# Tree attention on one core: K and Q of 40 more heads are regrouped by GpSimd before they are transposed, and ScalarE takes over eight V copies

## The chip, the cores and the metric

The kernel runs on one core of one Trainium2 chip. The metric is the device time of one execution in microseconds (us); lower is better. A core has five engines that run their own instruction streams and meet at semaphores: TensorE (PE in the profile; its weight loads are PEld), VectorE (DVE), ScalarE (ACT), GpSimd (POOL) and SyncE (SP). Transfers between the chip's memory and the core's on-chip memory are started by an engine (here nearly all by GpSimd) and carried by 16 DMA engines.

## The reference

The inputs Q, K and V have shape 8 x 12 x 512 x 64 (float32), so there are 96 heads of 512 rows. The 512 positions are the nodes of a binary heap, and a query may look at itself and at its ancestors only:

```python
for i in range(seq):
    mask[i, i] = 1
    parent = i
    while parent > 0:
        parent = (parent - 1) // 2
        mask[i, parent] = 1
scores = np.einsum('bhqd,bhkd->bhqk', Q, K) * scale + (1 - mask) * (-1e9)
weights = np.exp(scores - np.max(scores, axis=-1, keepdims=True))
weights = weights / (np.sum(weights, axis=-1, keepdims=True) + 1e-10)
return np.einsum('bhqk,bhkd->bhqd', weights, V).astype(np.float32)
```

## The kernel before

**Tiling.** A query has at most nine ancestors, so the kernel does not compute 512 x 512 scores. The keys are put in an order in which one tile of 128 keys holds the top of the tree (`scores1`, L507) and four further tiles hold what single groups of queries can see (`scores2`, L566). The mask is not added: code vectors of keys and queries are multiplied into the same PSUM sum first, so that a forbidden pair comes out very negative. The 96 heads are worked on as 48 pairs, i = 0 to 47. The pairs from i = 8 on are "wide": their K and Q were loaded with two heads in one transfer row, and two pairs (four heads) are transposed together.

**One step.** The main loop (L796) has one step for each i. Its order of work is written out by hand: the strings of `FIRST` (L792) for steps 0 to 8, then "SVK" in odd steps and "SVQ" in even ones. S is `scores1` and `scores2` of pair i: matmuls on TensorE and exponentials on ScalarE (L529 or L525 for the first tile, then L560 or L586). V is `values` of pair i-1 (L592, matmuls on L605 into the tile `ob`), followed by `norm` (L644): a reciprocal (L651) and a multiplication (L653) on VectorE. `ob` has one buffer, so the next `values` waits until `norm` is done. K and Q are `turn` (L497): TensorE transposes four heads of K or Q, and VectorE copies the result from PSUM (three copies for K on L470, L474 and L478, one for Q on L493). A turn runs some four pairs ahead of the scores that use it.

**Two ways to transpose.** K and Q come in blocks of 8 heads, b = 0 to 11. `turn_slot` (L437) transposes one of eight slots of a group of four heads. Where a block is not "laid", it issues two transposes with 64 columns of weights each (L450), straight from the loaded tile. Where it is laid, GpSimd has copied the two heads of a pair side by side into a tile `besideK` or `besideQ` (`lay`, L426, one copy for each of the two groups of a block, L433), and one transpose with 128 columns of weights does (L441). `besideK` and `besideQ` have one buffer for each group: the copy for the next block waits until TensorE has read the group. `LAID` (L139) lists the laid blocks: 8 to 11, heads 64 to 95.

**The order inside `values`.** For each pair there are 20 matmuls: 12 with 128 columns of weights ("firsts" and "wholes") and 8 with 64 columns ("halves"). Up to i = 27 the halves come last (L637 on). From i = `4 * LAID[0] - 4` = 28 they stand between firsts and wholes (L630).

**V.** V comes in blocks of 16 heads, o = 0 to 5. Its rows are rearranged from the loaded tile `vst` into `vt` by many small copies (`spread`, L311, all on L364). From o = 2 on, VectorE does the parts A, B, C and E (table `BY_VECTOR`, L733, one a step), and GpSimd does X, N, Z0, Z1 (`spread_pool`) and the four "top" parts 6 to 9 (`spread_top`, L369). ScalarE has a table of its own, `BY_SCALAR` (L754), used for o = 0 and 1 only; its copies come at the end of a step, behind the exponentials of that step.

**GpSimd's queue.** `pool_program` (L676) is one list, which GpSimd works through strictly in order: loads (`load_k` and `load_q` through L256 or L244, `load_rows` L285, `load_leaves` L294), copies, lays and stores (L662). `ready` (L712) only decides behind which step of the main loop an entry is put into the program. An entry that has to wait holds up everything behind it in the list. The loads convert float32 to bfloat16 on the way. The last four heads are stored by SyncE (L826).

Of the kernel before, what the change touches and what calls it, by code (L numbers as in the profile page):

```python
# [119 lines left out]
def kernel(  # L120
# [7 lines left out]
    nc = tc.nc  # L128
# [7 lines left out]
    WIDE = 8  # L136
    KB, VB, VO = 8, 16, 16
    EIGHT = 2
    LAID = (8, 9, 10, 11)  # L139
    assert NH % VB == 0  # L140

    fp32 = mybir.dt.float32
# [90 lines left out]
    issued = {(name, h) for name in ("kst", "qst") for h in (0, 1)}  # L233
# [35 lines left out]
    def head(i, a):  # L269

        return 2 * i + a if i < WIDE else 4 * (i // 2) + i % 2 + 2 * a
# [151 lines left out]
    def slots(st, i):  # L423
        return st[2 * i // KB].rearrange("p (g x) t d -> p g (x t) d", x=2)

    def lay(name, b):  # L426

        st = {"kst": ksts, "qst": qsts}[name][b]
        assert all((name, h) in issued for h in range(KB * b, KB * b + KB))
        laid[name, b] = two = beside[name[0].upper()]  # L430
        for g in range(KB // 4):
            src = st[:, 4 * g:4 * g + 4, :, :].rearrange("p (a x) t d -> p (x t) a d", x=2)
            nc.gpsimd.tensor_copy(  # L433
                out=two[:, g, :, :, :].bitcast(int32), in_=src.bitcast(int32)
            )

    def turn_slot(dst, name, i, s, out):  # L437

        two = laid.get((name, 2 * i // KB))
        if two is not None:  # L440
# [5 lines left out]
            return  # L446
        assert 2 * i // KB not in LAID
        st = slots({"kst": ksts, "qst": qsts}[name], i)
# [143 lines left out]
    def values(i):  # L592

        if i < NP - 1:
            obs[i] = ob = psO.tile([P, 2, 512], fp32, name="ob")
        else:
            obs[i] = ob = psS.tile([P, 2, 512], fp32, name="s1")
        e1, e2, vt = ets[i], e2s[i % NE], vts[(head(i, 0) // VB) % NV]

        vtile = VTILE if i < WIDE else WVTILE  # L600
        parts = EIGHT_PARTS if head(i, 0) >= VB * EIGHT else PARTS[i >= WIDE]
        assert all(("vt", n, head(i, a)) in issued for n in parts for a in range(2))

        def product(e, a, t, tile_v, lo=0, hi=128, **flags):
            nc.tensor.matmul(  # L605
                out=ob[lo:hi, a, 65 * t:65 * t + 65],
                lhsT=e[:, a, PLACE[t], lo:hi],
                rhs=vt[vtile[tile_v][0]][:, head(i, a) % VB, vtile[tile_v][1], 0:D + 1],
                **flags,
            )  # L610

        def firsts(a):
            for t in range(4):
                product(e1, a, t, 0, start=t == 0, stop=False)

        def halves(a, last=True):
            for t in (0, 1):
                product(e2, a, t, 1 + SELF[t], 0, 64, start=False, stop=last and t == 1)
                product(e2, a, t, 1 + t, 64, 128, start=False, stop=last and t == 1)

        def wholes(a, last=False):
            for t in (2, 3):
                product(e2, a, t, 1 + t, start=False, stop=last and t == 3)

        if i == NP - 1:
            for a in range(2):
                firsts(a)
                wholes(a)
                halves(a)
        elif i >= 4 * LAID[0] - 4:  # L630
            for a in range(2):
                firsts(a)
            for a in range(2):
                halves(a, False)
            for a in range(2):
                wholes(a, True)
        else:  # L637
            for a in range(2):
                firsts(a)
                wholes(a)  # L640
            for a in range(2):
                halves(a)
# [33 lines left out]
    def pool_program():  # L676

        ops = [
            (load_k, 2, 2), (load_q, 2, 2), (load_v, 0, 4), (load_v, 4, 4),
            (load_k, 4, 4), (load_q, 4, 4), (load_k, 8, 4),  # L680
            (load_q, 8, 4), (load_v, 8, 8), (load_k, 12, 4),
            (load_q, 12, 4), (load_k, 16, 8), (load_q, 16, 4), (load_rows, 1, "upper"),
            (load_rows, 1, "even"), (load_rows, 1, "odd"), (load_q, 20, 4),
            (load_k, 24, 8), (load_q, 24, 8), (load_rows, 2, "upper"),
            (load_k, 32, 8), (load_leaves, 2, 0), (load_leaves, 2, 1),
            (load_q, 32, 8), (load_rows, 3, "upper"),
            (spread_pool, (1, "Z0", 8, 16), (1, "Z1", 8, 16)),
            (load_k, 40, 8), (load_q, 40, 8), (load_leaves, 3, 0), (load_leaves, 3, 1),
            (spread_top, 2, 0, 16), (spread_pool, (2, "Z0", 0, 16), (2, "Z1", 0, 16)),
            (load_q, 48, 8), (spread_pool, (2, "X", 0, 16)),  # L690
            (load_k, 48, 8), (spread_pool, (2, "N", 0, 16)),
            (load_rows, 4, "upper"), (spread_top, 3, 0, 16),
            (load_k, 56, 8), (load_q, 56, 8), (load_leaves, 4, 0), (load_leaves, 4, 1),
            (spread_pool, (3, "X", 0, 16), (3, "N", 0, 16), (3, "Z0", 0, 16), (3, "Z1", 0, 16)),
            (load_k, 64, 8), (store_rows, 0, 2), (load_q, 64, 8), (store_rows, 2, 4),
            (load_k, 72, 8), (spread_top, 4), (store, nc.gpsimd, 4, 12), (lay, "kst", 8),
            (load_q, 72, 8), (spread_pool, (4, "X", 0, 16), (4, "N", 0, 16)),
            (lay, "qst", 8), (load_rows, 5, "upper"),
            (spread_pool, (4, "Z0", 0, 16), (4, "Z1", 0, 16)),
            (load_leaves, 5, 0), (load_leaves, 5, 1), (load_k, 80, 8), (load_q, 80, 8),  # L700
            (store, nc.gpsimd, 16, 8), (lay, "kst", 9), (load_k, 88, 8), (load_q, 88, 8),
            (lay, "qst", 9), (store, nc.gpsimd, 24, 8), (store, nc.gpsimd, 32, 16),
            (spread_top, 5), (lay, "kst", 10), (store, nc.gpsimd, 48, 16), (lay, "qst", 10),
            (spread_pool, (5, "X", 0, 16), (5, "N", 0, 16)),
            (spread_pool, (5, "Z0", 0, 16), (5, "Z1", 0, 16)),
            (lay, "kst", 11), (store, nc.gpsimd, 64, 8), (lay, "qst", 11),
            (store, nc.gpsimd, 72, 8), (spread_leaves, 5, 1),
            (store, nc.gpsimd, 80, 8), (store, nc.gpsimd, 88, 4),
        ]
        return ops  # L710
# [36 lines left out]
    for o in range(EIGHT, NH // VB):  # L747
# [6 lines left out]
    BY_SCALAR = {  # L754
# [8 lines left out]
    }  # L763

    def spread_by(copy, table, i):

        for args in table.get(i, []):
            spread(copy, *args)

    program = pool_program()  # L770

    def pool(i):
# [23 lines left out]
    for i in range(NP + 1):  # L796
        steps = FIRST[i] if i < len(FIRST) else "SVK" if i % 2 else "SVQ"
        for step in steps:
            if step == "S" and i < NP:
                scores1(i)  # L800
                scores2(i)
            if step == "V" and i >= 1:
                values(i - 1)
                norm(i - 1)
                valued = True
            if step == "K" and kdone < NP:
                kdone = turn("kst", kdone)
            if step == "Q" and qdone < NP:
                qdone = turn("qst", qdone)
            if step == "W":  # L810
                nc.scalar.copy(
                    out=codes[64:64 + CODE_ROWS, 1280:1536], in_=codes[0:CODE_ROWS, 1280:1536]
                )
            if step == "X":
                spin("s1" if valued else "ob", 2)
            if step == "D":
                spread_by(nc.vector.tensor_copy, BY_VECTOR, i)
            if step == "A":
                spread_by(nc.scalar.copy, BY_SCALAR, i)
        if "D" not in steps:  # L820
            spread_by(nc.vector.tensor_copy, BY_VECTOR, i)
        if "A" not in steps:
            spread_by(nc.scalar.copy, BY_SCALAR, i)
        pool(i)
# [32 lines left out]
```

## Time and profile before

| what | value |
|---|---|
| median of 3 runs | 133.66 us (133.48 to 133.95) |
| the profiled execution, its own time | 133.8 us |
| its span, first to last instruction | 131.9 us |
| instructions | 5281 |
| TensorE clock granted, mean | 0.978 |
| copies of V on GpSimd (L364), 32x512 and 32x1024 | 22 and 16 |
| lay copies (L433) | 16 |

The page of the profile names an instruction by its engine and line; "out<-in" are the program's tiles. "Busy" is the time in which an engine executes; "idle before" is how long it stood still ahead of the instruction, with what ended the wait. A timeline row is: start, duration, engine, line, operation, tiles, shape, and how many instructions were merged into the row; the duration then reaches from the start of the first to the end of the last. Matmuls overlap, so the time that a group of matmuls costs TensorE is read from the start of one group to the start of the next. The difference between the execution's time and its span (1.9 us) lies outside the instructions.

### The profile page before, as it was taken

The page shows a single profiled execution, that of the slowest core. Times are in us where ns is not written, and L with a number is a line of the kernel's source. Part 1 is how long each engine was busy: PE and PEld are TensorE (multiplying, and loading weights), DVE is VectorE, ACT ScalarE, POOL GpSimd, SP SyncE. Part 2 cuts the span into 40 slices and gives each one's busy share as a digit, 9 for nine tenths or more (in the row PEclk, how much of TensorE's full clock was granted, in tenths as well). Part 3 has the DMA queues.
Part 4 walks back from the last instruction along what each step waited for, and adds up shares of the span by engine and source line. Part 5 has one row for each costly group of instructions (what it writes and reads, how often), then busy time and mean ns, then how long its engine had stood idle before and what let it go on. Part 6 is the DMA issues. An engine that isn't in the chain of part 4 may idle for free.

```text
span 131.9 us, 5281 instructions
## 1 busy us (share of the span) xinstructions
PE 114.7 (87%) x2286; PEld 80.4 (61%) x2289; DVE 108.8 (82%) x261; ACT 94.4 (72%) x153; POOL 87.1 (66%) x118
## 2 busy tenths in 40 slices
PE   6883999999789699899899999999988999999920
PEld 2351576676566476666577677677765766776610
DVE  3438569988999989989999999999999999877350
ACT  4358268989768957968858787787868668688900
POOL 6994624245623998799951899999999977802200
PEclk9999599999999999999999999999999999999996
DMA  3999999999999999999999999999999999999984
GB/s 122 216 190 196 198 199 205 199 199 207 206 200 205 204 202 208 209 202 205 202 208 204 244 236 305 338 204 207 203 288 285 228 391 406 400 402 402 397 315 148
DMA packets 29719, 32.28 MB, mean 245 GB/s; under 512 B 1488, under 2 KB 26704, under 8 KB 29696
## 3 DMA queue, kind: packets, MB, share of 16 engines
q0 software_dynamic: 28416, 30.68, 115.2%
q1 hardware_dynamic: 864, 0.93, 2.1%
q10 hardware_dynamic: 416, 0.33, 1.0%
q8 instruction: 18, 0.29, 0.8%
q14 instruction: 5, 0.04, 0.1%
HBM read 37.96 MB, written 12.58 MB: 383 GB/s over the span
## 4 chain that ended last, share of the span: by engine, by line
DVE 38%; PE 24%; DMA 14%; POOL 10%; issue 5%; ACT 3%; ACTq 1%; POOLq 0%
DVE of L653 12%; DVE vt L364 11%; DMA kst<-in_K_dram 8%; PE ob L605 8%; DMA qst<-in_Q_dram 6%; POOL vt L364 5%; DVE rec L651 3%; PE s L511 3%; DVE kq L493 3%; DVE kq L470 3%; DVE kq L478 3%; DVE kq L474 3%; PE s L519 2%; ACT e L560 2%; PE s L544 1%
## 5 line engine op out<-in xcount | busy, mean ns | idle before, releaser
L529 ACT ACTIVATE e<-s 128x1024 bf16<-128x1024 f32 x40 | 40.9, 1023 | 20.7 <-PE s L519 20.1
L605 PE MATMUL ob<-vt,e 128*128 128x65 bf16 (+1 forms) x940 | 39.8, 198 | 6.0 <-DVE of L653 3.0
L605 PEld LDWEIGHTS <-e 128*128 128x128 bf16 (+1 forms) x960 | 31.7, 103 | 15.9 <-DVE of L653 5.1
L560 ACT ACTIVATE e<-s 128x384 bf16<-128x384 f32 x80 | 34.7, 491 | 0.0
L653 DVE TENSOR_TENSOR of<-ob,rec 128x512 f32<-128x512 f32 x47 | 32.5, 691 | 1.6
L364 POOL COPY vt<-vst 32x512 int32<-32x512 int32 (+1 forms) x38 | 31.0, 816 | 2.9 <-PE ob L605 1.2
L364 DVE COPY vt<-vst 32x1024 bf16<-32x1024 bf16 (+6 forms) x54 | 26.8, 497 | 2.3 <-DMA vst<-in_V_dram 1.3
L662 POOL DMA_DIRECT2D out_dram<-of x13 | 12.1, 928 | 12.7 <-DVE of L653 9.2
L511 PE MATMUL s<-codes 40*128 40x512 bf16 x96 | 19.3, 398 | 0.7 <-ACT e L525 0.4
L519 PE MATMUL s<-kq 64*128 64x512 bf16 x96 | 18.5, 380 | 0.0
L651 DVE RECIPROCAL rec<-ob 128x8 f32<-128x8 f32 x47 | 9.6, 204 | 8.8 <-PE ob L605 8.0
L554 PEld LDWEIGHTS <-kq 64*128 64x128 bf16 x320 | 12.1, 94 | 4.8
L554 PE MATMUL s<-kq 64*128 64x160 bf16 (+1 forms) x320 | 14.6, 208 | 0.0
L544 PE MATMUL s<-codes 40*128 40x384 bf16 x80 | 13.6, 333 | 0.3
L493 DVE COPY kq<-qtp 128x1024 bf16<-128x1024 bf16 x20 | 13.6, 681 | 0.0
L256 POOL DMA_DIRECT2D qst<-in_Q_dram x11 | 8.3, 752 | 6.8 <-DMA vst<-in_V_dram 2.6
L525 ACT ACTIVATE e<-s 128x1024 bf16<-128x1024 f32 x8 | 8.2, 1022 | 6.0 <-PE s L519 5.9
L544 PEld LDWEIGHTS <-codes 40*128 40x128 bf16 x80 | 6.1, 94 | 7.9 <-issue 1.2
L256 POOL DMA_DIRECT2D kst<-in_K_dram x10 | 7.6, 760 | 3.9 <-PE ob L605 2.8
L470 DVE COPY kq<-ktp 128x256 bf16<-128x256 bf16 x20 | 8.3, 415 | 0.3 <-PE ktp L450 0.3
L474 DVE COPY kq<-ktp 128x256 bf16<-128x256 bf16 x20 | 8.3, 415 | 0.0
L478 DVE COPY kq<-ktp 128x512 bf16<-128x512 bf16 x20 | 8.3, 414 | 0.0
(49 smaller groups left out, 139.4 us busy)
## 6 DMA issues: line engine op xcount, KB each, us to landing
kst<-in_K_dram POOLq DMA_DIRECT2D x10, 512.0 KB, 13.2
out_dram<-of POOLq DMA_DIRECT2D x5, 1024.0 KB, 13.9
qst<-in_Q_dram POOLq DMA_DIRECT2D x9, 512.0 KB, 14.5
out_dram<-of POOLq DMA_DIRECT2D x2, 2048.0 KB, 20.8
vst<-in_V_dram POOLq DMA_DIRECT2D x12, 256.0 KB, 14.9
vst<-in_V_dram POOLq DMA_DIRECT2D x6, 512.0 KB, 14.3
out_dram<-of POOLq DMA_DIRECT2D x1, 1536.0 KB, 10.7
qst<-in_Q_dram POOLq DMA_DIRECT2D x5, 256.0 KB, 11.9
```

Source lines behind the costliest of these rows:

```text
L256: return nc.gpsimd.dma_start(out=kept[b][:, h0 % KB:h0 % KB + n, :, :].rearrange("p (g x) t d -> p g (x t d)", x=2), in_=wide[:, h0 // 2:( ...
L364: return copy(out=dst, in_=src)
L493: nc.vector.tensor_copy(out=qq[:, :, 0:16, :].rearrange("p b u c -> p b (u c)"), in_=halves)
L511: nc.tensor.matmul(out=sp[:, a, :], lhsT=(k1code if i < WIDE else k1wide)[64 * a:64 * a + CODE_ROWS, :], rhs=(q1code[64 * a:64 * a + CODE_ ...
L519: nc.tensor.matmul(out=sp[:, a, :], lhsT=keys(i, a, TOP), rhs=qTs[i][64 * a:64 * a + 64, :, :].rearrange("p t c -> p (t c)"), start=False, ...
L529: ) if i < WIDE else nc.scalar.activation(
L544: nc.tensor.matmul(out=flat[:, a, :, :].rearrange("p u (t c) -> p u t c", t=4)[:, :, :, 16:64], lhsT=k2wide[64 * a:64 * a + CODE_ROWS, :], ...
L554: nc.tensor.matmul(out=flat[:, a, :, lo:hi], lhsT=keys(i, a, WTILE2[t]), rhs=qT[64 * a:64 * a + 64, :, lo:hi], start=False, stop=t == 1, s ...
L560: nc.scalar.activation(out=e2s[i % NE][:, a, :, 32:128].rearrange("p t (r u) -> p t r u", u=2), in_=flat[:, a, :, :].rearrange("p u (t r) ...
L605: nc.tensor.matmul(out=ob[lo:hi, a, 65 * t:65 * t + 65], lhsT=e[:, a, PLACE[t], lo:hi], rhs=vt[vtile[tile_v][0]][:, head(i, a) % VB, vtile ...
L651: nc.vector.reciprocal(out=rec[:, a:a + n, :, :], in_=o4[:, a:a + n, :, D:D + 1])
L653: nc.vector.tensor_tensor(out=ofs[g][:, first:last + 1:step, :, :], in0=o4[:, a:a + n, :, 0:D], in1=rec[:, a:a + n, :, :].to_broadcast([P, ...
```

## The change

`LAID` takes in the blocks 2, 3, 4, 5 and 7 (heads 16 to 47 and 56 to 63); block 6 stays as it is. For each new block the program has a K lay and a Q lay, each of two copies; the Q lay of block 2 is split into its two halves, with other entries between. A new constant `LATE` = 28 keeps the order inside `values` where it was. The eight top copies of o = 2 and 3 leave GpSimd's list, and `BY_SCALAR` gives them to ScalarE, one a step in steps 12 to 15 and 18 to 21. Where GpSimd issued the load of K of heads 72 to 79, it now issues Q of the same heads directly behind it, ahead of the lay of block 7, the top copies of o = 4 and the store of heads 4 to 15; the copies of V of o = 4 are spread out between the loads and lays behind them.

```diff
--- before.py
+++ after.py
@@ -136,7 +136,8 @@
     WIDE = 8
     KB, VB, VO = 8, 16, 16
     EIGHT = 2
-    LAID = (8, 9, 10, 11)
+    LAID = (2, 3, 4, 5, 7, 8, 9, 10, 11)
+    LATE = 28
     assert NH % VB == 0
 
     fp32 = mybir.dt.float32
@@ -423,12 +424,12 @@
     def slots(st, i):
         return st[2 * i // KB].rearrange("p (g x) t d -> p g (x t) d", x=2)
 
-    def lay(name, b):
+    def lay(name, b, g0=0, g1=2):
 
         st = {"kst": ksts, "qst": qsts}[name][b]
-        assert all((name, h) in issued for h in range(KB * b, KB * b + KB))
+        assert all((name, h) in issued for h in range(KB * b + 4 * g0, KB * b + 4 * g1))
         laid[name, b] = two = beside[name[0].upper()]
-        for g in range(KB // 4):
+        for g in range(g0, g1):
             src = st[:, 4 * g:4 * g + 4, :, :].rearrange("p (a x) t d -> p (x t) a d", x=2)
             nc.gpsimd.tensor_copy(
                 out=two[:, g, :, :, :].bitcast(int32), in_=src.bitcast(int32)
@@ -627,7 +628,7 @@
                 firsts(a)
                 wholes(a)
                 halves(a)
-        elif i >= 4 * LAID[0] - 4:
+        elif i >= LATE:
             for a in range(2):
                 firsts(a)
             for a in range(2):
@@ -681,23 +682,26 @@
             (load_q, 8, 4), (load_v, 8, 8), (load_k, 12, 4),
             (load_q, 12, 4), (load_k, 16, 8), (load_q, 16, 4), (load_rows, 1, "upper"),
             (load_rows, 1, "even"), (load_rows, 1, "odd"), (load_q, 20, 4),
-            (load_k, 24, 8), (load_q, 24, 8), (load_rows, 2, "upper"),
-            (load_k, 32, 8), (load_leaves, 2, 0), (load_leaves, 2, 1),
-            (load_q, 32, 8), (load_rows, 3, "upper"),
-            (spread_pool, (1, "Z0", 8, 16), (1, "Z1", 8, 16)),
-            (load_k, 40, 8), (load_q, 40, 8), (load_leaves, 3, 0), (load_leaves, 3, 1),
-            (spread_top, 2, 0, 16), (spread_pool, (2, "Z0", 0, 16), (2, "Z1", 0, 16)),
-            (load_q, 48, 8), (spread_pool, (2, "X", 0, 16)),
+            (load_k, 24, 8), (load_q, 24, 8), (load_rows, 2, "upper"), (lay, "kst", 2),
+            (load_k, 32, 8), (lay, "qst", 2, 0, 1), (load_leaves, 2, 0), (load_leaves, 2, 1),
+            (load_q, 32, 8), (lay, "qst", 2, 1, 2), (load_rows, 3, "upper"),
+            (spread_pool, (1, "Z0", 8, 16), (1, "Z1", 8, 16)), (lay, "kst", 3),
+            (load_k, 40, 8), (load_q, 40, 8), (lay, "qst", 3),
+            (load_leaves, 3, 0), (load_leaves, 3, 1), (lay, "kst", 4),
+            (spread_pool, (2, "Z0", 0, 16), (2, "Z1", 0, 16), (2, "X", 0, 16)),
+            (load_q, 48, 8), (lay, "qst", 4),
             (load_k, 48, 8), (spread_pool, (2, "N", 0, 16)),
-            (load_rows, 4, "upper"), (spread_top, 3, 0, 16),
-            (load_k, 56, 8), (load_q, 56, 8), (load_leaves, 4, 0), (load_leaves, 4, 1),
+            (load_rows, 4, "upper"), (lay, "kst", 5),
+            (load_k, 56, 8), (load_q, 56, 8), (lay, "qst", 5),
+            (load_leaves, 4, 0), (load_leaves, 4, 1),
             (spread_pool, (3, "X", 0, 16), (3, "N", 0, 16), (3, "Z0", 0, 16), (3, "Z1", 0, 16)),
-            (load_k, 64, 8), (store_rows, 0, 2), (load_q, 64, 8), (store_rows, 2, 4),
-            (load_k, 72, 8), (spread_top, 4), (store, nc.gpsimd, 4, 12), (lay, "kst", 8),
-            (load_q, 72, 8), (spread_pool, (4, "X", 0, 16), (4, "N", 0, 16)),
-            (lay, "qst", 8), (load_rows, 5, "upper"),
+            (load_k, 64, 8), (store_rows, 0, 2), (load_q, 64, 8), (store_rows, 2, 3),
+            (lay, "kst", 7), (store_rows, 3, 4),
+            (load_k, 72, 8), (load_q, 72, 8), (lay, "qst", 7), (spread_top, 4),
+            (store, nc.gpsimd, 4, 12), (spread_pool, (4, "X", 0, 16)), (load_rows, 5, "upper"),
+            (lay, "kst", 8), (spread_pool, (4, "N", 0, 16)), (lay, "qst", 8),
+            (load_leaves, 5, 0), (load_leaves, 5, 1), (load_k, 80, 8), (load_q, 80, 8),
             (spread_pool, (4, "Z0", 0, 16), (4, "Z1", 0, 16)),
-            (load_leaves, 5, 0), (load_leaves, 5, 1), (load_k, 80, 8), (load_q, 80, 8),
             (store, nc.gpsimd, 16, 8), (lay, "kst", 9), (load_k, 88, 8), (load_q, 88, 8),
             (lay, "qst", 9), (store, nc.gpsimd, 24, 8), (store, nc.gpsimd, 32, 16),
             (spread_top, 5), (lay, "kst", 10), (store, nc.gpsimd, 48, 16), (lay, "qst", 10),
@@ -761,6 +765,9 @@
         9: [(1, 6, 8, 16)],
         12: [(1, 9, 8, 16)],
     }
+    for o in (2, 3):
+        for j in range(4):
+            BY_SCALAR.setdefault(6 * o + j, []).append((o, 6 + j, 0, VB))
 
     def spread_by(copy, table, i):
 
```

## The prediction

> **What bounds the kernel now.** I read the page first (engines, slices, transfers), then busy times by stretch, then the timeline of single steps.
>
> ```profile
> PE 114.7 (87%) x2286; PEld 80.4 (61%) x2289; DVE 108.8 (82%) x261; ACT 94.4 (72%) x153; POOL 87.1 (66%) x118
> ...
> DMA  3999999999999999999999999999999999999984
> ...
> HBM read 37.96 MB, written 12.58 MB: 383 GB/s over the span
> ```
>
> No engine is full over the whole span, but the DMA engines are: nine tenths or more in every slice but the first and the last two. Reads and writes together are 50.5 MB, and the change alters none of them. So one bound is the traffic: it can end sooner only by what the tail wastes (below).
>
> ```profile
> 31.90:52.70 20.80, 17.98 (x415) 13.06 (x414) 19.83 (x46) 15.70 (x28) 13.62 (x19) 1.00 1.30 204
> 52.70:71.50 18.80, 17.43 (x408) 12.59 (x406) 17.79 (x43) 14.33 (x25) 14.23 (x18) 1.00 1.27 205
> 71.50:89.40 17.90, 17.31 (x380) 12.73 (x376) 17.29 (x42) 14.28 (x24) 16.36 (x22) 1.00 1.20 261
> 89.40:108.60 19.20, 17.94 (x344) 13.00 (x342) 18.59 (x41) 14.33 (x25) 17.80 (x25) 1.00 1.19 266
> ```
>
> Columns: stretch, its length, busy PE, PEld, DVE, ACT, POOL, clock, DMA share, GB/s. These are steps 8 to 40, in four eights. VectorE is busy 19.83 of 20.80, 17.79 of 18.80, 17.29 of 17.90 and 18.59 of 19.20 us: 95 to 97% everywhere. It is the bound of the compute, with TensorE close behind. Compute and traffic end together, so both must be followed.
>
> ```profile
> 68.60 0.21 DVE L651 RECIPROCAL rec<-ob 128x8 f32<-128x8 f32 x1
> ...
> 73.00 0.21 DVE L651 RECIPROCAL rec<-ob 128x8 f32<-128x8 f32 x1
> ```
>
> Two steps lie between these rows. VectorE runs without a gap there and no V copy is stretched: 73.00 - 68.60 = 4.40 us for a Q step and a K step.
>
> ```profile
> 69.59 0.79 PE L605 MATMUL ob<-vt,e 128*128 128x65 bf16 x20
> 70.21 0.61 PE L450 MATMUL ktp<-ptile,kst 128*64 128x128 bf16 x16
> 70.76 0.40 PE L511 MATMUL s<-codes 40*128 40x512 bf16 x2
> ...
> 85.24 0.89 PE L605 MATMUL ob<-vt,e 128*128 128x65 bf16 x20
> 85.97 0.61 PE L441 MATMUL qtp<-ptile,besideQ 128*128 128x128 bf16 x8
> 86.51 0.40 PE L511 MATMUL s<-codes 40*128 40x512 bf16 x2
> ```
>
> From start to start: values 0.62 us and an unlaid turn 0.55 in step 23; values 0.73 and a laid turn 0.54 in step 30.
>
> **The change part by part.**
>
> *Laid turns on TensorE.* Blocks 2 to 5 and 7 have two K and two Q turns each: 5 x 4 = 20 turns change from 16 narrow transposes to 8 full ones. The rows say that this saves 0.01 us a turn: nothing. It costs something instead. Values in step 30 take 0.73 - 0.62 = 0.11 us more for the same 20 matmuls, and the one difference is their order: halves in the middle, hence one more change between 128 and 64 columns of weights. In the new turns the order stays (LATE), so the halves come last and the full turn follows them: the same extra change, now between values and turn. I take 0.10 us a turn, 20 x 0.10 = 2.0 us on TensorE. The Trainium skill, page "TensorEngine Tiling (Array Packing)", section "Key Properties", states that a change of tiling mode drains TensorE; it gives no time for it. It speaks against this change, and the 0.11 us agrees with it.
>
> Is it on the path? Two steps of TensorE without a wait are 2 x (0.62 + 0.55 + scores). With scores of 69.59 - 68.64 = 0.95 (the L511 that opens step 23 stands in the row below) that is 4.24 us, and 4.44 with the extra changes.
>
> ```profile
> 68.64 0.40 PE L511 MATMUL s<-codes 40*128 40x512 bf16 x2
> ```
>
> VectorE needs 4.40 with no V copy stretched and 4.68 at their mean of 0.56 (next part), so it hides the turns: 0, with 2.0 as the upper end if that cover is gone.
>
> *GpSimd's copies.* Added: 20 lay copies, 10 of K and 10 of Q. Removed: 8 top copies of 32x512.
>
> ```profile
> L364 POOL COPY vt<-vst 32x512 int32<-32x512 int32 x22 | 13.8, 626 | 2.2 <-PE ob L605 1.2
> ...
> L433 POOL COPY besideQ<-qst 128x512 int32<-128x512 int32 x8 | 5.3, 680 | 0.2
> ...
> L433 POOL COPY besideK<-kst 128x512 int32<-128x512 int32 x8 | 4.7, 612 | 1.1 <-PE ktp L441 0.9
> ```
>
> 10 x 0.680 + 10 x 0.612 - 8 x 0.626 = 12.9 - 5.0 = 7.9 us more copying. What that does to VectorE is the main term.
>
> ```profile
> 48.64 1.03 POOL L364 COPY vt<-vst 32x1024 int32<-32x1024 int32 x1
> 48.97 0.98 DVE L364 COPY vt<-vst 32x1024 bf16<-32x1024 bf16 x1
> ...
> 70.16 0.42 DVE L364 COPY vt<-vst 32x1024 bf16<-32x1024 bf16 x1
> ...
> L364 DVE COPY vt<-vst 32x1024 bf16<-32x1024 bf16 x29 | 16.3, 560 | 0.5
> ```
>
> Alone, a V copy takes 0.42 us (70.16). When GpSimd is copying it lasts until 0.28 after GpSimd's end: 48.97 + 0.98 = 49.95 against 48.64 + 1.03 = 49.67. The last row is the group between 31.9 and 108.6 us: 29 copies at 0.560, so 29 x 0.14 = 4.1 us of stretching. In the same time GpSimd copied:
>
> ```profile
> 31.90:108.60 76.70, 20.27 (x38) 1.53 (x4) 28.60 (x34) 1.00 1.24 233
> ...
> 31.90:108.60 76.70, 8.74 (x14) 1.00 1.24 233
> ```
>
> 28.60 us of V (third busy column of the first row) and 8.74 of lays (second row), 37.3 us. That is 4.1 / 37.3 = 0.11 us of VectorE for each us of copying; 7.9 x 0.11 = **0.87 us**, on the engine that is the bound. Lower end: the eight removed copies were those that hurt (rival 2). Upper end: each of 20 lays meets a V copy and holds it for half of its length, 20 x 0.32 = 6.4, far off, as there is one V copy in about 2.2 us.
>
> The Trainium skill, page "SBUF — State Buffer", section "Who interferes with whom", states that VectorE in its two-port modes and GpSimd share a port pair by an exclusive lock, held for the whole instruction by whichever came first. By that rule a lay of 0.65 is met with a chance of 0.65 / 2.2 and costs half its length, 0.10; 20 x 0.10 less 8 x 0.09 is an estimate of 1.2 us where the rows give 0.87. The row at 48.97 agrees with the rule.
>
> *ScalarE's copies.* Eight copies of 32x512, one a step, each between two exponentials:
>
> ```profile
> 31.39 0.62 ACT L364 COPY vt<-vst 32x512 int32<-32x512 int32 x1
> 31.92 1.01 ACT L529 ACTIVATE e<-s 128x1024 bf16<-128x1024 f32 x1
> ...
> 42.40 1.02 ACT L529 ACTIVATE e<-s 128x1024 bf16<-128x1024 f32 x1
> ...
> 52.74 1.02 ACT L529 ACTIVATE e<-s 128x1024 bf16<-128x1024 f32 x1 [0.68 <-PE s L519]
> ...
> 57.86 1.02 ACT L529 ACTIVATE e<-s 128x1024 bf16<-128x1024 f32 x1 [1.25 <-PE s L519]
> 58.78 0.87 ACT L560 ACTIVATE e<-s 128x384 bf16<-128x384 f32 x2
> ...
> 67.26 1.02 ACT L529 ACTIVATE e<-s 128x1024 bf16<-128x1024 f32 x1 [1.13 <-PE s L519]
> ```
>
> A copy takes 31.92 - 31.39 = 0.53 from start to start, so a step of ScalarE becomes (58.78 - 57.86) + 0.87 + 0.53 = 2.32 us. Steps 12 to 15 last (52.74 - 42.40) / 4 = 2.59 each, steps 18 to 21 (67.26 - 57.86) / 4 = 2.35: longer. I take 0; upper end 8 x (2.32 - 2.12) = 1.6, if all went at TensorE's 2.12.
>
> *Order on GpSimd.* Every lay stands ahead of a turn on TensorE, and TensorE's matmuls are one stream, so a late lay stalls scores, values and everything behind. The tightest are those of block 8:
>
> ```profile
> 72.89 0.78 POOL L256 DMA_DIRECT2D kst<-in_K_dram  x1 [1.04 <-PE ob L605]
> ...
> 77.44 1.20 POOL L433 COPY besideK<-kst 128x512 int32<-128x512 int32 x2
> ...
> 79.39 2.21 POOL L364 COPY vt<-vst 32x1024 int32<-32x1024 int32 x2
> 81.67 1.38 POOL L433 COPY besideQ<-qst 128x512 int32<-128x512 int32 x2
> ...
> 83.77 0.44 PE L441 MATMUL ktp<-ptile,besideK 128*128 128x128 bf16 x5
> ```
>
> Ahead of the K lay now come the Q load (0.78, as the K load in the first row), the Q lay of block 7 (1.38), X (1.1, half of the 2.21) and a V load (0.78 again): 77.44 + 4.04 = 81.5, its first half done at 82.1, needed at 83.77. The Q lay follows with N between: 81.5 + 1.2 + 1.1 = 83.8, first half done at 84.5, needed at 85.97. The K lay of block 7 falls into idle time ahead of 72.89. So 1.5 us is left: cost 0. The Q load that moved 4.7 us ahead gains nothing: its lay waits for GpSimd's own list, not for the load.
>
> *The tail.* What a delay of compute does to the end:
>
> ```profile
> GB/s 328 328 328 230 98 164 131 131 197 98 197 344 393 369 377 385 369 401 369 377 393 328 156 123 123 107 25 25 25 0 0 0 0 0 0 0 0 0 0 0
> ...
> out_dram<-of SPq DMA_DIRECT2D x1, 512.0 KB, 3.6
> ```
>
> This is 127 to 132 us in slices of 0.125. The last store leaves when VectorE is done and needs 3.6 us; the rest of GpSimd's stores flows beside it until about 128.4. Later compute meets an emptier queue, so I pass on 0.75 of a delay (bounds 0.5 and 1). Earlier compute gains only the seven slices of about 150 where 390 is possible, 0.9 x 0.6 = 0.55 us.
>
> **Sum.** 0 + 0.87 + 0 + 0 = 0.87 us of compute, x 0.75 = 0.65. The profiled execution took 133.8 (span 131.9 and 1.9 around it), so 134.45; the median shown is 0.14 below it: **134.3 us**.
>
> **The rivals.**
> 1. *The traffic hides it.* The DMA engines are full to 127 us; if V copies meet fewer lays than their share and the delay stays under 0.5, the end moves by under 0.4: 133.66, no change. For: the full DMA row. Against: the last store waits for VectorE, not for the queue.
> 2. *Faster, because the eight removed copies were the harmful ones.* They ran at 43 to 46 and 53 to 56 us:
>
> ```profile
> 43.00:56.50 13.50, 3.85 (x6) 0.40 (x1) 9.17 (x12) 1.00 1.28 204
> ```
>
> Six V copies took 3.85 us instead of at most 6 x 0.42 = 2.52: 1.3 us of the 4.1 in a sixth of the time. If the lays fall between V copies, compute comes 1.3 us sooner, and the tail's 0.55 is what is left of it: 133.1. It decides once VectorE's stretching falls by 0.5 or more. Against: lays stand in the same stretch (blocks 4 and 5).
> 3. *TensorE becomes the bound.* At 4.44 against VectorE's 4.40 it nearly is. If the 2.0 us come through wholly, 133.7 + 2.0 = 135.7. Against: 4.40 holds only where no V copy is stretched.
> 4. *GpSimd is late.* If its list slips by the 1.5 us left and 1.0 more, block 8's first lay stalls TensorE by 1.0 on top of my 0.65: 135.3.
>
> **How the numbers follow.** Forecast 0.41, with 133.95 to 135.2 as its own range; rival 1 0.27; rival 2 0.17; rival 3 0.09; rival 4 0.06. A measurement of this kernel tells about 0.3% (0.4 us) from no change. Slower 0.41 + 0.09 + 0.06 = 0.56, same 0.27, faster 0.17. Range 132.9 to 135.7: from rival 2 with another 0.2 from its tail to rival 3.
>
> **What would show it.** Right: the 32x1024 V copies on VectorE rise above 0.560 us, VectorE stays 95% busy from 32 to 108 us, the L511 row follows a new L441 row 0.54 later and that row follows L605 by about 0.72, no L441 waits for L433, and the last store leaves at 128.3 instead of 127.4. Wrong: a mean of the V copies at or below 0.560 (rival 2), waits of VectorE for `ob` in steps 8 to 28 (rival 3), waits of L441 for `beside` (rival 4), or a DMA row with gaps, which would undo the bound of the traffic.

## The result and the profile after

The changed kernel takes 134.86 us (median of 16 runs, 134.13 to 137.41), the kernel before 133.70 us (16 runs, 133.28 to 134.15). The ratio is 1.0089 [1.0066, 1.0113]: slower by 1.2 us, where the prediction said 0.65. The profiled execution took 134.39 us with a span of 132.6. Ratios here and below leave disturbed (slow) runs out: three of the 16 after the change, and seven of the twelve of one experiment, e5_unread, whose median is therefore not given. Lines from L364 on stand one further down than before (L364 is now L365, L605 L606, L653 L654, L662 L663).

The page of the kernel after: busy times, granted clock, DMA share, traffic.

```profile
PE 114.6 (86%) x2126; PEld 80.4 (61%) x2129; DVE 111.3 (84%) x261; ACT 99.0 (75%) x161; POOL 94.0 (71%) x130
...
PEclk9999999999999999999999999999999999999997
DMA  3999999999999999999999999999999999999954
...
HBM read 37.96 MB, written 12.58 MB: 381 GB/s over the span
```

VectorE has the same 261 instructions as before and 2.5 us more busy time (111.3 against 108.8). GpSimd has 94.0 instead of 87.1. TensorE has 160 matmuls fewer and the same busy time. The DMA row is a little weaker at the end: 5 and 4 in the last slices instead of 8 and 4.

Busy time by stretch, kernel after, in the windows of the prediction (length, PE, PEld, DVE, ACT, POOL, clock, DMA share, GB/s):

```profile
31.90:52.70 20.80, 17.59 (x315) 12.49 (x315) 19.68 (x44) 16.53 (x30) 16.60 (x24) 1.00 1.30 204
52.70:71.50 18.80, 17.72 (x358) 12.57 (x357) 17.80 (x41) 16.93 (x29) 14.79 (x20) 1.00 1.27 205
71.50:89.40 17.90, 16.32 (x319) 11.95 (x316) 17.32 (x38) 13.55 (x23) 16.71 (x23) 1.00 1.21 262
89.40:108.60 19.20, 18.31 (x352) 13.33 (x351) 18.59 (x41) 14.33 (x26) 17.80 (x23) 1.00 1.19 269
```

VectorE is still 95 to 97% busy everywhere, with fewer instructions in the same time. So its instructions have become longer. Which ones, the groups of VectorE between 31.9 and 108.6 us say (kernel after, shapes kept apart):

```profile
L365 DVE COPY vt<-vst 32x1024 bf16<-32x1024 bf16 x28 | 16.8, 600 | 0.5
```

The V copies take 0.600 us instead of 0.560. To see the whole loss, both kernels are cut at their own steps 8 and 40 (from 0.45 us ahead of the first exponential of step 8 to the first exponential of step 40, so every stretch holds 32 steps and 0.45 us). First the kernel before: the V copies of VectorE, ScalarE and GpSimd, then the lays of GpSimd.

```profile
31.47:108.58 77.11, 20.32 (x38) 1.96 (x4) 28.60 (x34) 1.00 1.24 233
...
31.47:108.58 77.11, 8.72 (x14) 1.00 1.24 233
```

The same of the kernel after:

```profile
30.44:110.08 79.64, 22.84 (x38) 6.87 (x12) 23.49 (x26) 1.00 1.24 237
...
30.44:110.08 79.64, 18.86 (x31) 1.00 1.24 237
```

These 32 steps became 79.64 - 77.11 = 2.53 us longer, and VectorE's 38 V copies 22.84 - 20.32 = 2.52 us longer. What is left of the stretch, 56.79 and 56.80 us, did not move. GpSimd copied 23.49 + 18.86 = 42.35 us instead of 37.32.

The timelines say what held VectorE. Every stretched V copy of these stretches ends 0.1 to 0.3 us behind the end of a GpSimd instruction. Sorted by the kind of that instruction, what the 38 copies took beyond 0.42 us (0.28 for those of 32x512) comes to 2.7 us behind V copies, 0.3 behind lays and 2.0 behind issues of transfers in the kernel before, and to 4.3, 1.9 and 1.5 in the kernel after. So the lays hold VectorE 1.5 us longer than before. GpSimd's V copies hold it 1.5 us longer too, although there are eight fewer, and the issues 0.5 less.

One collision, VectorE first and then GpSimd, kernel after:

```profile
82.19 1.09 DVE L365 COPY vt<-vst 32x1024 bf16<-32x1024 bf16 x1
...
87.17 1.11 DVE L365 COPY vt<-vst 32x1024 bf16<-32x1024 bf16 x1
```

```profile
81.96 1.04 POOL L365 COPY vt<-vst 32x1024 int32<-32x1024 int32 x1
...
86.97 2.21 POOL L365 COPY vt<-vst 32x1024 int32<-32x1024 int32 x2
```

Both V copies start 0.2 us after one of GpSimd's and take 1.1 us instead of 0.42. These are not lays: they are N, and Z0 with Z1, of V block o = 4, which the new order has put elsewhere.

Of the 2.53 us, only 1.2 arrive at the end. Two things stand between. The first is the start: step 8 begins at 30.44 us instead of 31.47. The profiled execution of the kernel before had a dip of the clock ahead of it (slice 5 of its page, 13.2 to 16.5 us):

```profile
PEclk9999599999999999999999999999999999999996
```

The steps of e3_scalar, e4_noleaf and e8_order, three variants of the kernel before whose profiles have no such dip, begin at 29.9 to 30.5 us. So the last store is late by 2.53 - 1.03 = 1.50 us in these two executions. It leaves SyncE as follows, first in the kernel before, then in the kernel after (there with the median time from issue to landing in the second row; the prediction shows 3.6 us for the kernel before).

```profile
127.41 0.39 SPq L662 DMA_DIRECT2D out_dram<-of  x1
```

```profile
128.91 0.39 SPq L663 DMA_DIRECT2D out_dram<-of  x1
...
out_dram<-of SPq DMA_DIRECT2D x1, 512.0 KB, 2.8
```

127.41 is 1.50 earlier than 128.91. The second thing is the end of the traffic. Before, the store needed 3.6 us and landed at 131.04; now it needs 2.8 and lands at 131.72, 0.68 later. The transfers of the kernel after from 128 to 132 us, in slices of 0.1:

```profile
DMA  9999822011000000003999999999999940000000
GB/s 451 369 451 451 328 82 82 0 41 41 0 0 0 0 0 0 0 0 133 348 389 410 358 410 399 369 389 389 369 399 379 358 144 0 0 0 0 0 0 0
```

From 128.5 us on there is only a trickle, and from 129.0 to 129.8 nothing moves: the queue had been worked off, and nothing was left until the last store came. The kernel before had no such gap between 127 us and its end. By these two profiles the change costs 1.50 - 0.82 = 0.7 us (0.82 being what the earlier store waited in the queue, 3.6 - 2.8), and with equal starts it would be 1.7; the medians, 1.2 apart, lie between.

### The profile page after: what moved, and what is told of

Its sections match the earlier page's. It is cut to its first block, busy times and chain, and to the rows that moved or that the text cites. A ratio compares the mean times of both kernels' runs of the same rounds, so it can differ in the third digit from the quotient of the medians.

```text
span 132.6 us, 4979 instructions
## 1 busy us (share of the span) xinstructions
PE 114.6 (86%) x2126; PEld 80.4 (61%) x2129; DVE 111.3 (84%) x261; ACT 99.0 (75%) x161; POOL 94.0 (71%) x130
## 4 chain that ended last, share of the span: by engine, by line
DVE 57%; PE 15%; DMA 9%; POOL 9%; issue 5%; ACT 1%; ACTq 1%; POOLq 0%
DVE of L654 17%; DVE vt L365 17%; DMA qst<-in_Q_dram 9%; PE ob L606 6%; DVE kq L494 6%; DVE rec L652 5%; DVE kq L471 4%; DVE kq L479 4%; DVE kq L475 4%; POOL kst L245 2%; PE s L512 2%; POOL vst L245 2%; POOL qst L245 2%; PE qtp L442 2%; PE s L520 1%
## 5 line engine op out<-in xcount | busy, mean ns | idle before, releaser
L606 PE MATMUL ob<-vt,e 128*128 128x65 bf16 (+1 forms) x940 | 39.3, 197 | 7.0 <-DVE of L654 4.0
L606 PEld LDWEIGHTS <-e 128*128 128x128 bf16 (+1 forms) x960 | 31.3, 102 | 16.6 <-DVE of L654 5.9
L654 DVE TENSOR_TENSOR of<-ob,rec 128x512 f32<-128x512 f32 x47 | 32.5, 692 | 1.6
L365 DVE COPY vt<-vst 32x1024 bf16<-32x1024 bf16 (+6 forms) x54 | 29.4, 545 | 2.4 <-DMA vst<-in_V_dram 1.5
L365 POOL COPY vt<-vst 32x1024 int32<-32x1024 int32 (+1 forms) x30 | 25.9, 864 | 1.5
L663 POOL DMA_DIRECT2D out_dram<-of x13 | 12.1, 929 | 11.1 <-DVE of L654 9.2
L434 POOL COPY besideK<-kst 128x512 int32<-128x512 int32 x18 | 10.8, 620 | 2.3 <-PE ktp L442 1.5
L365 ACT COPY vt<-vst 32x512 int32<-32x512 int32 (+3 forms) x21 | 11.1, 529 | 0.7 <-DMA vst<-in_V_dram 0.2
L442 PE MATMUL qtp<-ptile,besideQ 128*128 128x128 bf16 x144 | 11.1, 220 | 0.6 <-POOL besideQ L434 0.4
L434 POOL COPY besideQ<-qst 128x512 int32<-128x512 int32 x18 | 11.2, 643 | 0.3
L442 PE MATMUL ktp<-ptile,besideK 128*128 128x128 bf16 x144 | 11.0, 219 | 0.3 <-DVE kq L479 0.3
```

Source lines behind the costliest of these rows:

```text
L365: return copy(out=dst, in_=src)
L434: nc.gpsimd.tensor_copy(out=two[:, g, :, :, :].bitcast(int32), in_=src.bitcast(int32))
L442: nc.tensor.transpose(out=out(dst), in_=two[:, 2 * i % KB // 4, s, :, :].rearrange("p a d -> p (a d)"), identity=ptile[:, 0:128],)
L606: nc.tensor.matmul(out=ob[lo:hi, a, 65 * t:65 * t + 65], lhsT=e[:, a, PLACE[t], lo:hi], rhs=vt[vtile[tile_v][0]][:, head(i, a) % VB, vtile ...
L654: nc.vector.tensor_tensor(out=ofs[g][:, first:last + 1:step, :, :], in0=o4[:, a:a + n, :, 0:D], in1=rec[:, a:a + n, :, :].to_broadcast([P, ...
```

## The experiments

**Theory A**: GpSimd's added copies hold VectorE's V copies, VectorE sets the length of the steps, and the traffic decides what of it arrives at the end. **Rival B**: the full turns cost TensorE time. **Rival C**: ScalarE's eight copies do it. A fourth question is what the new order on GpSimd costs, and a fifth what a gain of compute would have been worth.

The measurements together. The columns: GpSimd's copying (V and lays) in steps 8 to 40, busy time of VectorE's V copies there, length of these steps, the difference of the two, issue and landing of the last store, median and ratio to the kernel before.

| kernel | GpSimd | V copies | steps 8-40 | rest | last store | landed | median | ratio |
|---|---|---|---|---|---|---|---|---|
| before | 37.32 | 20.32 | 77.11 | 56.79 | 127.41 | 131.04 | 133.70 | 1 |
| after | 42.35 | 22.84 | 79.64 | 56.80 | 128.91 | 131.72 | 134.86 | 1.0089 [1.0066, 1.0113] |
| e2_nocopy | 33.04 | 21.19 | 78.35 | 57.16 | 128.33 | 131.14 | 134.01 | 1.0027 [1.0000, 1.0054] |
| e3_scalar | 31.30 | 19.49 | 76.94 | 57.45 | 125.55 | 131.28 | 133.70 | 1.0000 [0.9978, 1.0022] |
| e5_unread | 43.20 | 22.95 | 79.63 | 56.68 | 129.04 | 131.85 | - | 1.0068 [1.0030, 1.0106] |
| e8_order | 36.61 | 21.14 | 77.69 | 56.55 | 127.23 | 131.03 | 133.61 | 1.0011 [0.9992, 1.0030] |
| e7_tops | 47.77 | 22.06 | 85.22 | 63.16 | 134.44 | 137.25 | 138.91 | 1.0384 [1.0361, 1.0407] |
| e9_tops_unread | 47.96 | 23.98 | 81.23 | 57.25 | 129.85 | 132.68 | 135.52 | 1.0146 [1.0121, 1.0172] |

The columns from "GpSimd" to "landed" are of one profiled execution each. The last store depends on when the steps begin, too: the stretch starts at 31.47 us in the kernel before and at 31.15 in e2_nocopy, whose profiled execution had the same dip of the clock, and at 29.79 to 30.46 in the others.

**e2_nocopy**: the kernel after, without 16 of the 20 new lay copies (blocks 3, 4, 5 and 7). Their full turns read what block 2 left in the tiles, so the output of these heads is another.

```diff
-        for g in range(g0, g1):
+        for g in range(g0, g1) if b == 2 or b >= 8 else ():
```

> The changed kernel with 16 of the 20 new lay copies left out (blocks 3, 4, 5 and 7): their turns stay full transposes and read the K and Q of block 2, so the scores of heads 24 to 47 and 56 to 63 are those of other heads. Theory A: GpSimd copies less than before the change, so 133.1 to 133.5 us, mean V copy under 0.55 us. Theory B: the 20 full turns are still there, 134.5 us or more.

134.01 us, 1.0027 [1.0000, 1.0054]. Of the 1.2 us about 0.8 went with the copies; A asked for all of it, and B for none. The steps of e2_nocopy (V copies, then lays):

```profile
31.15:109.50 78.35, 21.19 (x38) 6.87 (x12) 23.45 (x26) 1.00 1.24 236
...
31.15:109.50 78.35, 9.59 (x15) 1.00 1.24 236
```

The lays fell by 18.86 - 9.59 = 9.27 us and the V copies by 22.84 - 21.19 = 1.65: 0.18 us of VectorE for each us of lays. Leaving lays out also moves everything behind them in GpSimd's list, so this is the effect of both.

**e5_unread**: the kernel after with all its lays in their places, but nobody reads the 20 new ones. The turns of blocks 2 to 5 and 7 are narrow as before. This removes the full turns alone.

```diff
-        laid[name, b] = two = beside[name[0].upper()]
+        two = beside[name[0].upper()]
+        if b >= 8:
+            laid[name, b] = two
...
-        assert 2 * i // KB not in LAID
```

The copies go into `besideK` and `besideQ` as in the kernel after. Spare tiles for them (planned as e1_spare, which gave no time) don't fit into the core's on-chip memory beside the rest.

> The changed kernel, but nobody reads the 20 new lay copies: they are made at the same places, and the turns of blocks 2 to 5 and 7 stay as before (16 narrow transposes each). Theory A (the lay copies stretch VectorE's V copies): as the changed kernel, 134.4 to 135.1 us. Theory B (TensorE's extra change of weight width, or waits for the lays): back to before, 133.4 to 133.9 us.

1.0068 [1.0030, 1.0106], and 134.61 us for the profiled execution. That is nearer to the time of the change (134.39 for its profiled execution) than to that of the kernel before. The five runs behind this ratio lie between 133.59 and 135.58 us, so the time alone doesn't decide; the steps do:

```profile
30.32:109.95 79.63, 22.95 (x38) 6.87 (x12) 23.63 (x26) 1.00 1.24 235
```

79.63 us for the 32 steps against 79.64, with V copies at 22.95 against 22.84. The last store leaves at 129.04 against 128.91. Without a single new full turn nothing comes back. B falls.

**e3_scalar**: the kernel before with the eight top copies given to ScalarE, and nothing else.

```diff
-            (spread_top, 2, 0, 16), (spread_pool, (2, "Z0", 0, 16), (2, "Z1", 0, 16)),
+            (spread_pool, (2, "Z0", 0, 16), (2, "Z1", 0, 16)),
...
-            (load_rows, 4, "upper"), (spread_top, 3, 0, 16),
+            (load_rows, 4, "upper"),
...
+    for o in (2, 3):
+        for j in range(4):
+            BY_SCALAR.setdefault(6 * o + j, []).append((o, 6 + j, 0, VB))
```

> The kernel before with one part of the change alone: ScalarE makes the eight top copies of o = 2 and 3, no block is laid anew, no order is changed. Theory A: 5.0 us less copying on GpSimd, V copies shorter by 0.5 to 1.5 us in all; of it the tail of the traffic lets through at most 0.55, so 133.1 to 133.5 us. Theory C (ScalarE's eight copies delay the exponentials): 134.0 us or more, and TensorE waiting for exponentials in steps 12 to 21.

133.70 us, 1.0000 [0.9978, 1.0022]. C's loss did not come, and neither did A's gain. Steps and last store of e3_scalar:

```profile
29.93:106.87 76.94, 19.49 (x38) 6.87 (x12) 23.38 (x26) 1.00 1.25 228
...
125.55 0.39 SPq L662 DMA_DIRECT2D out_dram<-of  x1
...
out_dram<-of SPq DMA_DIRECT2D x1, 512.0 KB, 5.7
```

The V copies fell by 0.83 us, but the steps by 0.17 only: the rest of them grew by 0.66 us, of which 0.5 is VectorE waiting longer for TensorE's `ob` (1.2 us instead of 0.7). The last store leaves 1.86 us sooner than in the kernel before, 1.54 of it because the steps began sooner (29.93 us instead of 31.47). It then needs 5.7 us instead of 3.6 and lands no sooner. The lead ended in the queue.

A store this early hides small delays too, so the time of e3_scalar alone can't clear ScalarE. Two others do: in the kernel after, with the same eight copies on ScalarE, the rest of the steps is 56.80 us as against 56.79 before, and e7_tops and e9_tops_unread (below), which take these copies off ScalarE, are slower and not faster. C falls.

**e4_noleaf** and **e6_noleaf** ask what any relief of VectorE could bring. They leave out VectorE's parts A, B, C and E of V blocks 2 to 5 (28 copies; the output of these heads is another), e4_noleaf in the kernel before, e6_noleaf in the kernel after.

```diff
-            spread(copy, *args)
+            if args[0] >= EIGHT and args[1] in ("A", "B", "C", "E"):
+                needs(args[1], *args[0:1], *args[2:], "leaf")
+            else:
+                spread(copy, *args)
```

> The kernel before with VectorE's copies of the V parts A, B, C and E left out for o = 2 to 5, so the values of heads 32 to 95 use rows of earlier heads. VectorE loses about 15 us of work. The bound by traffic: the DMA engines were full already, so the end moves by about 0.55 us, to 133.1 us. If traffic is no bound: the compute goes at TensorE's 4.24 us for two steps instead of 4.8, and the kernel ends near 125 to 127 us.

> The changed kernel with VectorE's copies of the V parts A, B, C and E left out for o = 2 to 5, so the values of heads 32 to 95 use rows of earlier heads. All lays, full turns and ScalarE copies stay. Theory A: what the lays stretched is gone, the last store leaves before 127 us and the traffic ends the kernel as in the kernel before, 133.4 to 133.9 us. Theory B or C (full turns, ScalarE's copies): TensorE or ScalarE keep it above 134.3 us.

e4_noleaf: 133.60 us, 1.0011 [0.9984, 1.0037]. e6_noleaf: 133.32 us, 0.9988 [0.9972, 1.0004]. The page of e4_noleaf and its last store:

```profile
PE 113.3 (86%) x2286; PEld 80.3 (61%) x2289; DVE 94.0 (71%) x233; ACT 94.4 (72%) x153; POOL 85.5 (65%) x118
...
DMA  4999999999999999999999999999999999999992
...
123.47 0.39 SPq L662 DMA_DIRECT2D out_dram<-of  x1
...
out_dram<-of SPq DMA_DIRECT2D x1, 512.0 KB, 7.5
```

VectorE lost 14.8 us of work (94.0 instead of 108.8). The steps became 2.1 us shorter (75.04 instead of 77.11). TensorE is then busy for all of the 25.0 us from 80 to 105, so it is the likely next bound. The last store left 3.9 us sooner, 1.5 of it from an earlier start of the steps, and it landed at 130.93, 0.1 us sooner than in the kernel before. The DMA row is full to the last slice but one. In the kernel after, the same cut removes the whole loss: the store leaves at 125.68 and lands at 130.96. So the traffic ends at about 131.0 us however early compute is done, and the table reads: a last store issued by 127.4 lands at 130.9 to 131.3, and one issued from 128.3 on lands 2.8 us after its issue. The two lines meet at 131.0 - 2.8 = 128.2. Up to there lateness is free, and behind it each us counts in full. No profile has its last store between 127.41 and 128.33, so the corner itself is worked out, not seen.

**e8_order**: the kernel before with only the new order from the load of Q of heads 72 to 79 on.

```diff
-            (load_k, 72, 8), (spread_top, 4), (store, nc.gpsimd, 4, 12), (lay, "kst", 8),
-            (load_q, 72, 8), (spread_pool, (4, "X", 0, 16), (4, "N", 0, 16)),
-            (lay, "qst", 8), (load_rows, 5, "upper"),
-            (spread_pool, (4, "Z0", 0, 16), (4, "Z1", 0, 16)),
+            (load_k, 72, 8), (load_q, 72, 8), (spread_top, 4),
+            (store, nc.gpsimd, 4, 12), (spread_pool, (4, "X", 0, 16)), (load_rows, 5, "upper"),
+            (lay, "kst", 8), (spread_pool, (4, "N", 0, 16)), (lay, "qst", 8),
             (load_leaves, 5, 0), (load_leaves, 5, 1), (load_k, 80, 8), (load_q, 80, 8),
+            (spread_pool, (4, "Z0", 0, 16), (4, "Z1", 0, 16)),
```

> The kernel before with one part of the change alone: Q of heads 72 to 79 and the loads behind it stand in the new order, no block is laid anew, no copy goes to ScalarE. All theories: nothing, 133.4 to 133.9 us. If the order of the loads mattered: beyond 0.4 us to either side.

133.61 us, 1.0011 [0.9992, 1.0030]: no change. Its steps all the same:

```profile
30.46:108.15 77.69, 21.14 (x38) 1.97 (x4) 28.24 (x34) 1.00 1.24 232
```

The V copies grew by 0.82 us with no copy added on any engine. Where, the timelines of VectorE and GpSimd in e8_order show:

```profile
82.59 0.92 DVE L364 COPY vt<-vst 32x1024 bf16<-32x1024 bf16 x1
...
87.49 1.02 DVE L364 COPY vt<-vst 32x1024 bf16<-32x1024 bf16 x1
```

```profile
82.19 1.04 POOL L364 COPY vt<-vst 32x1024 int32<-32x1024 int32 x1
...
87.19 2.21 POOL L364 COPY vt<-vst 32x1024 int32<-32x1024 int32 x2
```

N (82.19) and Z0 (87.19) now begin just ahead of V copies, the same two collisions as in the kernel after. Alone this is hidden, since the last store still leaves at 127.23.

**e7_tops**: the kernel after with the eight top copies back on GpSimd, so the same lays on a longer list.

```diff
+            (spread_top, 2, 0, 16),
             (spread_pool, (2, "Z0", 0, 16), (2, "Z1", 0, 16), (2, "X", 0, 16)),
...
-            (load_rows, 4, "upper"), (lay, "kst", 5),
+            (load_rows, 4, "upper"), (spread_top, 3, 0, 16), (lay, "kst", 5),
...
-    for o in (2, 3):
-        for j in range(4):
-            BY_SCALAR.setdefault(6 * o + j, []).append((o, 6 + j, 0, VB))
```

> The changed kernel with the eight top copies of o = 2 and 3 back on GpSimd, ahead of Z0 and Z1 of o = 2 and behind the V load of o = 4. Theory A: 5.0 us more copying on GpSimd, 0.5 to 1.5 us more stretching, and GpSimd nearer to its deadlines: 135.2 to 136.4 us. Theory C (ScalarE's copies are what costs): at or below 134.4 us.

138.91 us, 1.0384 [1.0361, 1.0407]: far more than A expected, and not by stretching. Its V copies take 22.06 us, less than in the kernel after, but the rest of the steps is 63.16 instead of 56.80 (the profiled execution, 139.92 us, is the slowest of the five):

```profile
30.39:115.61 85.22, 22.06 (x38) 1.97 (x4) 28.55 (x34) 0.96 1.21 228
```

TensorE's waits in e7_tops (total, times, longest), and GpSimd's timeline ahead of the longest:

```profile
PE qtp L442 <- POOL besideQ L434: 5.2, 5, 3.1
```

```profile
44.33 5.88 POOL L365 COPY vt<-vst 32x512 int32<-32x512 int32 x7
50.16 0.76 POOL L257 DMA_DIRECT2D qst<-in_Q_dram  x1
50.97 1.16 POOL L434 COPY besideQ<-qst 128x512 int32<-128x512 int32 x2
```

Copies fill GpSimd from 44.33 on, and the Q lay that TensorE needs comes 3.1 us late. With this wait comes a second loss, as the page of e7_tops shows:

```profile
PEclk9999999999999975799999999999999999999996
```

The granted clock is down in slices 15 to 17 (the trace has it at 0.50 from 50.3 to 57.1 us), beginning within this wait, and the next values take 55.40 - 54.27 = 1.13 us instead of 0.72. The profile of e9_tops_unread (below), without the wait, has no such dip. Late lays are rival 4 of the prediction, in another place. The kernel after has one such wait for a Q lay, ahead of step 8:

```profile
PE qtp L442 <- POOL besideQ L434: 0.4, 1, 0.4
```

**e9_tops_unread**: e7_tops with the 20 new lays unread, as in e5_unread. Nobody waits for them; their copying stays.

> As e7_tops (all 20 new lay copies made, the eight top copies back on GpSimd), but nobody reads the 20 copies: the turns of blocks 2 to 5 and 7 stay narrow and can't wait for them. If the 5 us that e7_tops lost are waits of TensorE for late lays (rival 4 of the prediction): most of them are gone, 134.5 to 136 us, where only the stretching is left. If they are stretching of VectorE's V copies: near 138.9 us again.

135.52 us, 1.0146 [1.0121, 1.0172]. So 138.91 - 135.52 = 3.4 us of e7_tops were late lays with what followed them, and 135.52 - 133.70 = 1.8 us remain. Its steps:

```profile
29.79:111.02 81.23, 23.98 (x38) 1.96 (x4) 28.50 (x34) 1.00 1.24 238
```

The rest, 57.25, is normal again, and the V copies are up by 3.66 us against the kernel before, the highest of all. With all lays and all top copies on GpSimd, VectorE is held longest.

## Why the prediction was right or wrong

**The bound: right, and stronger than said.** VectorE sets the steps: in seven of the eight kernels of the table their length less the V copies is 56.5 to 57.5 us. TensorE is close behind: without 28 V copies the steps get only 2.1 us shorter (e4_noleaf). The traffic sets the end: e4_noleaf and e6_noleaf show a floor at 131.0.

**Laid turns: right.** A new laid turn in the kernel after, TensorE's timeline:

```profile
60.54 0.79 PE L606 MATMUL ob<-vt,e 128*128 128x65 bf16 x20
61.26 0.62 PE L442 MATMUL ktp<-ptile,besideK 128*128 128x128 bf16 x8
61.81 0.40 PE L512 MATMUL s<-codes 40*128 40x512 bf16 x2
```

Values take 61.26 - 60.54 = 0.72 us and the turn 0.55; the prediction had named 0.72 and 0.54. The 0.10 us a turn is real: in this kernel, between 30 and 80 us, the values that the trace shows with all 20 matmuls take 0.72 us ahead of a full turn (median of 16) and 0.62 ahead of a narrow one (of 4). e5_unread shows that it is hidden. Rival 3 is out. The Trainium skill's rule on a change of tiling mode ("TensorEngine Tiling (Array Packing)", "Key Properties") fits the 0.72, but its cost had no place on the path. No run here shows that 64 columns of weights are such a mode.

**GpSimd's copies: the mechanism right, the size wrong.** This is the term that failed: 0.87 us forecast, 2.52 measured. The prediction multiplied more copying by a mean rate of 0.11; in these steps GpSimd copied 42.35 - 37.32 = 5.03 us more and VectorE lost 2.52, which is 0.50 for each us, so the amount of copying is not what sets the loss. Three parts can be told apart by single edits. (1) 9.27 us of lays cost 1.65 (after against e2_nocopy), 0.18 for each us instead of 0.11. The rate of 0.11 was a mean over the positions of the kernel before. There lays held VectorE for only 0.3 us in all (the sorting above), and two fifths of the stretching (2.0 of 5.0 us) stood behind issues of transfers and not behind copies. Lays in new places had no reason to meet V copies as seldom. (2) The removed top copies gave back 0.83 (e3_scalar) where 8 x 0.626 x 0.11 = 0.55 was counted. Rival 2 was right that they were harmful, though only 0.17 us came off the steps. (3) The new order cost 0.82 (e8_order), where the prediction counted nothing, since it looked only for late lays. If the parts add up, they make 1.65 - 0.83 + 0.82 = 1.64; the other 0.9 us come from no single edit here. The four lay copies of block 2 and new positions of everything behind them in the list are left for it, and which of these was not tried. The sorting of the stretched copies says only by what kind of instruction VectorE was held: 1.5 us more by lays, 1.5 more by V copies in new places, 0.5 less by issues. By the rule on the shared port pair that the Trainium skill states ("SBUF — State Buffer", "Who interferes with whom"), the estimate was 1.2: nearer, and still half. The rows at 82.19 and 87.17 agree with the rule itself.

**The tail: wrong in form.** Of a delay nothing passes until the last store leaves at 128.2, and then all of it; 0.75 of everything was neither. The kernel before had 0.8 us of this slack (128.2 - 127.41). A compute term too small by 2.52 - 0.87 = 1.65 and a slack that was not counted partly cancel: 0.65 against 1.2. That the forecast came this near is in part luck. The cap of a gain was given as 0.55 us; it is 0.1 (e4_noleaf lands at 130.93). Hence rival 2's 133.1 could not have come by way of VectorE, however many stalls went. The 0.55 was seven thin slices at 127 to 128 us. In e4_noleaf they are filled (123 to 132 us in slices of 0.225, so 127 to 128 are slices 18 to 22):

```profile
GB/s 382 419 401 419 382 473 364 401 364 346 437 401 382 414 369 423 423 373 405 360 341 369 369 346 328 278 255 132 100 105 105 77 27 9 0 0 0 0 0 0
```

The transfers ended no sooner all the same, so other slices were slower; why was not tried.

**ScalarE's copies: right**, nothing (the rest of the steps, 56.80 us against 56.79). That GpSimd is rid of them also does what the prediction didn't see: with them on its list the lays come late (e7_tops against e9_tops_unread, 3.4 us).

**Order: right for the time of this step alone** (e8_order) and for the lays of block 8, but incomplete: the V copies of block 4 landed on VectorE's, 0.82 us that the slack of the last store hid.

**What stays open.** e2_nocopy keeps about 0.4 us over the kernel before, at the edge of its interval. Its V copies (21.19 against 20.32) and its rest (57.16 against 56.79) are both a little longer; no run separates the two.

No version that beats the kernel before came out of this: e4_noleaf shows that even 14.8 us less work on VectorE gains nothing that can be measured.

## What to carry to other kernels

Price a copy that is put on GpSimd by the VectorE copies that it will meet, position by position, and do the same for every copy that a new order moves: the mean rate of the old order is no price for new places. Where the transfers are busy to the end, find, before a saving or a delay of compute is counted, the issue time of the last store at which the traffic is just done: up to there a delay counts nothing, behind it all, and a saving counts only as far as that time. And where an in-order list feeds deadlines, what is taken off it can matter more than what the taken work costs elsewhere.

## What the runs showed of the hardware that was not expected

GpSimd holds VectorE's V copies with more than copies. In the kernel before, VectorE and GpSimd:

```profile
99.84 1.05 DVE L364 COPY vt<-vst 32x1024 bf16<-32x1024 bf16 x1
```

```profile
99.52 1.15 POOL L662 DMA_DIRECT2D out_dram<-of  x1
```

GpSimd is issuing a store from 99.52 to 100.67, and a V copy of 0.42 us takes 1.05, ending 0.22 after the issue does. In the steps of this kernel six stretched V copies end behind an issue, at a cost of 2.0 us. Not every issue holds a copy: the V copy at 68.15 takes 0.42 us within the issue of a store from 68.10 to 69.18. What tells the two apart was not tried.

The runs of the changed kernel that its ratio uses also spread more, 134.13 to 136.06 us against 133.28 to 134.15. This fits the form of the tail: a kernel that has used up its slack passes on every delay of its start, such as the 1.03 us of the clock's dip above, which the kernel before absorbs. The granted clocks point the same way. After the change the four of these runs with a mean clock below 0.975 average 135.33 us and the nine with 0.98 or more 134.61, 0.72 apart; in the runs of the kernel before that stood beside the experiments it is 133.86 (16 runs) and 133.54 (30), 0.32 apart. No run changes the clock alone, so this stays an argument.
